# FOX projections of heads 0 to 3 in three panels of 512 features, and the inversions' column steps on GpSimd

## The chip, the core and the metric

The kernel runs on one core of one Trainium2 chip, in one launch. The metric is the device time of that launch in microseconds, as the median of several runs. The engines are TensorE (PE; its weight loads are listed as PEld), VectorE (DVE), ScalarE (ACT), GpSimd (POOL) and SyncE (SP). Each runs its own list of instructions in order and waits on semaphores for the others. DMAs are issued from SP's list (plain loads and stores) and from POOL's (loads that add to what is there).

## What is computed

One decoder block on x of 512 tokens by 1024 features. Two branches run in parallel from u = RMSNorm(x):

```python
proj = rmsnorm(x, g) @ w_in
# A, gated delta rule: 8 heads of 128; q, k, v through a causal conv of 4 and SiLU
#   a_mat = strictly lower part of (beta * k k^T * decay), per chunk
#   sol = triangular_solve(a_mat + eye, [v * beta, k * beta * exp(G)])   # unit lower triangular
#   then a scan over the chunks with state S
# B, forgetting attention (FOX): 8 heads of 128
#   q, k = rmsnorm per head;  p = softmax(q k^T / sqrt(d) + c_t - c_s), causal;  o_b = p v
merged = sigmoid(gate_a) * (y_a @ w_proj_gdn) + sigmoid(gate_b) * (o_b @ w_proj_fox)
h = x + merged @ w_out
out = h + square(relu(rmsnorm(h) @ w_up)) @ w_down
```

All is float32. Each large product is made of three: an operand is split into a high part (`hi`, rounded to the matmul's format) and the rest (`lo`), and hi.hi, lo.hi and hi.lo are added up in PSUM.

## The kernel before

Weights come in units of 128 x 1024 floats (512 KB), in the order of the list `seq`. `load` brings a unit by DMA, `prefetch_split` makes `hi` (ACT, 1.05 us) and `lo` (DVE, 1.22 us) of it, with four buffers for each, and `unit` hands it to the code that multiplies and starts the splits and loads of the next ones.

The stages follow one another: the gates, z and the first delta-rule group (heads 0 to 3, `gdn_group(0)`), the FOX projections of heads 0 to 3 (`fox_pair(0)`, `fox_pair(1)`), the second group (heads 4 to 7), a stream of products that are made by a scheme of seven instead of eight (`stream`, tile `st`, FOX heads 4 to 7 and the gates), the output projections, and the MLP (tile `mlp`), which takes the last 360 us. Small pieces of work run beside them as generators: `head`, `invert`, `scan`, `fox_worker`, `factors_u`. Each `tick()` in the big loops resumes every generator up to its next `yield`. What was written in this order is then put into each engine's list by a scheduler; it may move an instruction to another place in its engine's list, and that list is what the engine runs.

A FOX pair projects q and k of two heads and then v of both, in three panels of 256 features; a panel needs two units. For each block of 128 tokens the weights of TensorE are a block of u (128 x 128) and what streams through is a 256-wide piece of the unit: 24 products a block, 96 a panel, 576 for both pairs (tile `fx`, lines 961, 962, 964). One PSUM bank takes two blocks.

`invert` inverts, for 16 blocks (4 heads x 4 chunks) at once, the unit lower triangular matrices of a group. It starts with the 32 x 32 diagonal blocks: they are transposed on DVE into `E` (line 669), and 31 column steps follow (lines 681, 683): step j multiplies a column of E with a row of X into `tmp` and subtracts that from X, over r x n elements per partition with r = 31 - j and n = j // 2 + 1. Each step needs the one before. Then DVE transposes X back into `Xd` and `XT` (lines 689, 692), and TensorE multiplies the blocks together: `Qp` (line 707), `Tp` and `Tq`, `Q6` and `T6`. The step sizes in `INV_STEP` say how much work of the column steps goes between two ticks. The scan of the group needs the inverse.

POOL has the scalings of FOX q and k (line 889), the power that gives 1/sqrt (346), the masks (878), products for the decays, and the DMA issues of line 219, which add the second and later terms of the stream's and the MLP's weight sums to a buffer already loaded; each of them waits until DVE has made `lo` of what the buffer held.

Of the kernel before, what the change touches and what calls it, by code (L numbers as in the profile page):

```python
# [15 lines left out]
P = 128  # L16
T = 512
# [20 lines left out]
LA_NEW = 7  # L38
LA_RAW = 3
LA_SPLIT = 2  # L40
INV_STEP = (2500, 900)


def hybrid_block(tc, a, out):
# [21 lines left out]
    def nm(s):  # L66
        n_names[0] += 1
        return f"{s}_{n_names[0]}"
# [41 lines left out]
    def cs(c):  # L110
        return slice(c * P, (c + 1) * P)
# [123 lines left out]
    def prefetch_new(n):  # L235

        for m in range(pos[0], min(len(seq), n)):
            if fresh and m not in raws and seq[m][0] in FACTOR and FACTOR[seq[m][0]][1] is None and seq[m][1][0] != "w_st":
                load(m)
            if seq[m] in LONE and m not in begun:  # L240
                begin(m)

    def prefetch_split(n):
        while len(units) < min(len(seq), n):
            raw, cuts = raws[len(units)]
            hi = whl.tile([P, D], F32R, tag="hi", name=nm("hi"))
            if not units:
                h3 = v3(hi[:, 0:512], KT)
                r3 = v3(raw[:, 0:256], KT)
                act.copy(h3[:, :, 0:32], r3)  # L250
                vec.tensor_tensor(h3[:, :, 32:64], r3, h3[:, :, 0:32].bitcast(F32), op=ALU.subtract)
                units.append((hi, None))
                continue
            lo = whl.tile([P, D], F32R, tag="lo", name=nm("lo"))
            for c in cuts:
                act.copy(hi[:, c], raw[:, c])  # L256
                vec.tensor_tensor(lo[:, c], raw[:, c], hi[:, c].bitcast(F32), op=ALU.subtract)  # L257
            units.append((hi, lo))

    def unit(nme):  # L260
        n = pos[0]
        assert seq[n][0] == nme, (seq[n], nme)
        pos[0] += 1
        prefetch_split(n + 1 + LA_SPLIT)
        prefetch_raw(n + 1 + LA_RAW)
        prefetch_new(n + 1 + LA_NEW)
        return units[n]
# [391 lines left out]
    def invert(AT, rest, ahead):  # L659
# [9 lines left out]
        vec.transpose(E_[:, :].rearrange("p (c d i) -> p c d i", c=B, d=2),  # L669
                      dg[:, :].rearrange("p (i c) -> p c i", i=NI).unsqueeze(2).to_broadcast([P, B, 2, NI]))  # L670
        X_ = page(s="X")
        vec.tensor_copy(X_, x_id)
        yield
        E3 = v3(E_[:, :], B)
        X3 = v3(X_[:, :], B)
# [1 line left out]
        for j in range(B - 1):  # L677
            r, n = B - 1 - j, j // 2 + 1
            tmp = smp.tile([P, 144], F32, tag="tmp", name=nm("tmp"), bufs=2)
            t3 = tmp[:, 0:r * n].rearrange("p (a b) -> p a b", a=r)  # L680
            vec.tensor_tensor(t3, E3[:, j + 1:, j:j + 1].to_broadcast([P, r, n]),
                              X3[:, j:j + 1, 0:n].to_broadcast([P, r, n]), op=ALU.mult)
            vec.tensor_tensor(X3[:, j + 1:, 0:n], X3[:, j + 1:, 0:n], t3, op=ALU.subtract)
            w += 2 * (130 + r * n)
            if w > rest:
                w = 0
                yield
# [5 lines left out]
        Xd3 = v3(Xd[:, :], NI)  # L693
        XT3 = v3(XT[:, :], NI)

        X2 = sbp.tile([P, NI, 64], F32, tag="sub", name=nm("X2"))
        pool.memset(X2[0:32, :, 32:64], 0.0)
        act.copy(X2[0:32, :, 0:32], Xd3[0:32, :, :])
# [248 lines left out]
            act.copy(o, po)  # L947
            stores.append(start(store_late(obd[h], o)))

    def fox_pair(hp):  # L950
        vts = ([], [])
        for pn in range(3):
            us = [unit("w_fox"), unit("w_fox")]
            pg2 = [page(s="fqk"), page(s="fqk")]
            for t2 in range(2):
                ps = mmps("fx")
                for tb in (2 * t2, 2 * t2 + 1):
                    o = ps[:, (tb % 2) * 256:(tb % 2 + 1) * 256]
                    for k in range(KT):
                        w = us[k // 4][0][:, (k % 4) * 256:(k % 4 + 1) * 256]  # L960
                        mm(o, uhi[k][:, cs(tb)], w, start=(k == 0), stop=False)  # L961
                        mm(o, ulo[k][:, cs(tb)], w, start=False, stop=False)  # L962
                    for k in range(KT):
                        mm(o, uhi[k][:, cs(tb)], us[k // 4][1][:, (k % 4) * 256:(k % 4 + 1) * 256], start=False,  # L964
                           stop=(k == KT - 1))
                    if tb % 2 == 0:
                        tick()
                if pn < 2:
                    act.copy(pg2[t2], ps)
                else:  # L970
                    for j in range(2):
                        (vec.tensor_copy if j else act.copy)(
                            v3(pg2[j][:, 2 * t2 * P:(2 * t2 + 2) * P], 2), v3(ps[:, :], 2)[:, :, cs(j)])
                tick()
            if pn < 2:
                fq.append((2 * hp + pn, pg2, vts[pn]))
            else:
                for v, x in zip(vts, pg2):
                    v += [x[:, cs(c)] for c in range(NCH)]

    def stream(parts, other):

# [106 lines left out]
    start(decays(0, box, gt))  # L1089
    fws = [start(fox_worker())]  # L1090
    ch0 = gdn_group(0, box)
    fox_pair(0)
    fu = start(factors_u())
    fox_pair(1)
    start(decays(1, box, ch0))
    hold[0] = True
    for h in range(NZ1, H):
# [342 lines left out]
def _layout(inputs):  # L1440
# [18 lines left out]
    o["w_gdn"] = units(qkv)  # L1459
    o["conv"] = c(f["gdn_conv_w"][0].reshape(4, 3, H, P).transpose(3, 2, 1, 0).reshape(P, 24, 4))  # L1460
    fx = w[:, 4112:7184].reshape(D, 3, H, P)
    pan = []
    for hp in range(2):
        for h in (2 * hp, 2 * hp + 1):
            pan.append(np.concatenate([fx[:, 0, h], fx[:, 1, h]], axis=1))
        pan.append(np.concatenate([fx[:, 2, 2 * hp], fx[:, 2, 2 * hp + 1]], axis=1))
    o["w_fox"] = c(np.stack(pan).reshape(6, 2, 4, P, 256).transpose(0, 1, 3, 2, 4).reshape(12, P, D))
    q, k, v = [[fx[:, j, h] for h in range(H)] for j in range(3)]
    st = [np.concatenate(b, axis=1) for b in
          ((v[4], v[5], q[4], k[4]), (q[6], k[6], q[5], k[5]), (q[7], k[7], v[6], v[7]))]  # L1470
# [49 lines left out]
```

## Time and profile before

| what | value |
|---|---|
| median of 3 runs | 983.41 us (983.08 to 984.17) |
| span of the profiled execution, first to last instruction | 980.2 us |
| PE busy | 970.8 us, 99% |
| DVE busy | 710.9 us, 73% |
| ACT busy | 605.0 us, 62% |
| POOL busy | 240.2 us, 25% |
| clock granted to TensorE | full in every slice |
| FOX projections, heads 0 to 3 (`fx`) | from 122.1 to 213.3 us |
| column steps, group 0 and group 1 | 143.5 to 170.4 and 354.4 to 400.1 us, on DVE |

The profile is of one execution; its span ends with the last instruction, and the timed runs are about 3 us longer than it. A row of a group reads: line, engine, operation, output<-inputs with shapes, xcount, then the busy time in us and the mean duration in ns, then the idle time of the engine just before and what ended it. A row of a time line or of the chain reads: start in us, length in us, engine, and what ran. A row of the table by windows reads: window, its length, then busy us and number of instructions of each engine, the clock, the busy share of the DMA engines and GB/s. Matmuls are pipelined, so a recorded duration is longer than the distance from one to the next.

### The profile page before, as it was taken

The numbers are of one execution on the slowest core, as the hardware profiler recorded it, in microseconds if no ns is written. First come the engines' busy times: TensorE is split into PE (matmuls) and PEld (weight loads), VectorE is DVE, ScalarE is ACT, GpSimd is POOL, SyncE is SP. The second block draws the span as 40 slices with busy tenths as digits, with TensorE's granted clock in tenths as the row PEclk, the third lists the DMA queues.
The fourth block names the chain that finished last, engine by engine and source line by source line (L and its number), as shares of the span: only waits on it lengthen the run. The fifth ranks groups of instructions, "written<-read, shape, count | busy, mean of one in ns | idle before, by whom it ended". The sixth has DMA issues, their size and how long they took to land.

```text
span 980.2 us, 17198 instructions
## 1 busy us (share of the span) xinstructions
PE 970.8 (99%) x6545; PEld 874.8 (89%) x6545; DVE 710.9 (73%) x1204; ACT 605.0 (62%) x1050; POOL 240.2 (25%) x236
## 2 busy tenths in 40 slices
PE   8999999999999999999999999999999999999998
PEld 6788899998888999999999888889989989988986
DVE  6877778566577789855656535889896697698596
ACT  7766444766564787867656422678755765666761
POOL 1544120202533513522320005312121121121110
PEclk9999999999999999999999999999999999999999
DMA  7647662475437885757887735688798888889884
GB/s 266 213 135 223 174 158 90 130 239 181 129 116 228 189 166 141 197 129 166 236 201 215 273 103 171 125 181 173 190 188 196 187 173 206 181 175 202 186 166 119
DMA packets 93442, 174.38 MB, mean 178 GB/s; under 512 B 8016, under 2 KB 49200, under 8 KB 93360
## 3 DMA queue, kind: packets, MB, share of 16 engines
q1 hardware_dynamic: 78928, 120.85, 38.8%
q0 software_dynamic: 14432, 52.44, 30.5%
q8 instruction: 51, 0.84, 0.4%
q14 instruction: 31, 0.25, 0.1%
HBM read 152.25 MB, written 21.02 MB: 177 GB/s over the span
## 4 chain that ended last, share of the span: by engine, by line
PE 92%; DVE 4%; DMA 2%; ACT 1%; issue 1%; SPq 0%; DVEq 0%
PE mlp L1171 36%; PE st L1011 12%; PE mm L279 8%; PE mm L276 8%; PE mm L275 8%; PE fx L964 2%; PE fx L961 2%; PE fx L962 2%; PE fo L944 2%; PE sc L919 1%; PE pT L935 1%; DVE lo L257 1%; PE kk L639 1%; PE kq L647 1%; DMA ux<-ud 1%; PE v L797 1%
## 5 line engine op out<-in xcount | busy, mean ns | idle before, releaser
L1402 ACT CAST hi<-draw 128x1024 fp32r<-128x1024 f32 x124 | 130.0, 1050 | 118.4 <-PE mlp L1171 100.4
L1409 DVE TENSOR_TENSOR lo<-draw,hi 128x1024 fp32r<-128x1024 f32 x124 | 151.3, 1222 | 44.8 <-ACT hi L1402 41.6
L256 ACT CAST hi<-raw 128x1024 fp32r<-128x1024 f32 (+1 forms) x62 | 62.9, 1021 | 82.6 <-PE mm L276 59.5
L1171 PE MATMUL mlp<-hi,shi 128*128 128x512 f32 x280 | 109.5, 391 | 0.1
L1171 PE MATMUL mlp<-hi,slo 128*128 128x512 f32 x280 | 109.1, 390 | 0.0
L1171 PE MATMUL mlp<-lo,shi 128*128 128x512 f32 x280 | 109.0, 389 | 0.0
L257 DVE TENSOR_TENSOR lo<-raw,hi 128x1024 fp32r<-128x1024 f32 (+1 forms) x62 | 73.9, 1197 | 29.1 <-ACT hi L256 13.4
L1171 PE MATMUL mlp<-shi,lo 128*128 128x256 f32 x448 | 90.3, 283 | 0.0
L1171 PE MATMUL mlp<-slo,hi 128*128 128x256 f32 x448 | 90.3, 283 | 0.0
L1171 PE MATMUL mlp<-shi,hi 128*128 128x256 f32 x448 | 90.3, 283 | 0.0
L276 PE MATMUL mm<-ulo,hi 128*128 128x512 f32 x216 | 85.0, 394 | 1.2 <-DVE ulo L290 1.2
L275 PE MATMUL mm<-uhi,hi 128*128 128x512 f32 x216 | 85.0, 395 | 0.0
L257 DVE TENSOR_TENSOR lo<-sraw,hi 128x1024 fp32r<-128x1024 f32 x49 | 60.7, 1240 | 20.9 <-ACT hi L256 20.1
L1171 PEld LDWEIGHTS mlp<-shi,hi 128*128 128x128 f32 x448 | 70.6, 192 | 0.9
L1171 PEld LDWEIGHTS mlp<-shi,lo 128*128 128x128 f32 x448 | 69.9, 192 | 0.0
L1171 PEld LDWEIGHTS mlp<-slo,hi 128*128 128x128 f32 x448 | 69.8, 192 | 0.0
L256 ACT CAST hi<-sraw 128x1024 fp32r<-128x1024 f32 x49 | 51.3, 1047 | 26.6 <-PE st L1011 16.2
L1171 PEld LDWEIGHTS mlp<-hi,shi 128*128 128x128 f32 x280 | 52.6, 188 | 11.1 <-issue 0.7
L1171 PEld LDWEIGHTS mlp<-lo,shi 128*128 128x128 f32 x280 | 52.6, 188 | 11.1
L1171 PEld LDWEIGHTS mlp<-hi,slo 128*128 128x128 f32 x280 | 52.6, 188 | 10.3
L219 POOL DMA_DIRECT2D draw<-w_d x30 | 26.3, 876 | 129.9 <-DVE lo L1409 120.8
L219 POOL DMA_DIRECT2D draw<-w_u x32 | 27.7, 866 | 122.6 <-DVE lo L1409 120.0
(336 smaller groups left out, 2466.6 us busy)
## 6 DMA issues: line engine op xcount, KB each, us to landing
draw<-w_u POOLq DMA_DIRECT2D x32, 512.0 KB, 5.7
draw<-w_d POOLq DMA_DIRECT2D x32, 512.0 KB, 6.5
sraw<-w_st POOLq DMA_DIRECT2D x28, 512.0 KB, 5.9
draw<-w_d SPq DMA_DIRECT2D x26, 512.0 KB, 4.4
raw<-w_gdn SPq DMA_DIRECT2D x24, 512.0 KB, 3.8
draw<-w_u SPq DMA_DIRECT2D x24, 512.0 KB, 4.4
sraw<-w_st SPq DMA_DIRECT2D x21, 512.0 KB, 5.5
hd<-hd SPq DMA_DIRECT2D x34, 256.0 KB, 5.4
```

Of the source, the lines that this page charges most:

```text
L219: nc.gpsimd.dma_start(raw, a[w][c, q, s_], accum_op=ALU.add)
L256: act.copy(hi[:, c], raw[:, c])
L257: vec.tensor_tensor(lo[:, c], raw[:, c], hi[:, c].bitcast(F32), op=ALU.subtract)
L275: mm(o, w, rhi(k), start=(k == 0), stop=False)
L276: mm(o, w, rlo(k), start=False, stop=False)
L279: mm(o, lo[:, k * cols:(k + 1) * cols], rhi(k), start=False, stop=(k == KT - 1))
L944: mm(po[:, cs(i)], vt[c], st[i][:, cs(c)], start=(c == 0), stop=(c == i))
L961: mm(o, uhi[k][:, cs(tb)], w, start=(k == 0), stop=False)
L1011: mm(o, u, w, start=first and t == 0 and k == 0 and j == 0 and x is hi, stop=x is lo and k == 3, skip_group_check=True)
L1171: return (lambda *args, **kw: tc.keep_in_program_order(f(*args, **kw))) if self.pinned[0] else f
L1402: pact.copy(hi, raws[m][0])
L1409: pvec.tensor_tensor(lo, raws[m][0], hi[:, :].bitcast(F32), op=ALU.subtract)
```

## The change

The projections of FOX heads 0 to 3 are made in three panels of 512 features: q and k of heads 0 and 1; v of heads 0 to 3; q and k of heads 2 and 3. A panel needs four units, each now two k blocks by 512 features. Two PSUM banks are open at once, one for each of two blocks of 128 tokens; the four units are run through twice, once for each half of the tokens, so all four stay split until the second half has used them. `held` keeps `prefetch_split` from asking for more buffers than are free. A block of tokens takes 24 products of 512 features, a panel 96, all three 288. The bank of a block is copied out by ACT, in two pieces of 256 (q and k) or whole (v). The number of ticks stays 24. `factors_u` now starts after the first of three panels instead of after the first pair.

In `invert` both instructions of every column step go to GpSimd, the first copy of X goes to ACT, there is one more `yield` before `X2`, and the amount of steps between ticks is 1600 for both groups.

```diff
-INV_STEP = (2500, 900)
+INV_STEP = (1600, 1600)
...
+    held = [None]
+
     def prefetch_split(n):
-        while len(units) < min(len(seq), n):
+        while len(units) < min(len(seq), n, len(seq) if held[0] is None else held[0]):
...
         X_ = page(s="X")
-        vec.tensor_copy(X_, x_id)
+        act.copy(X_, x_id)
...
-            vec.tensor_tensor(t3, E3[:, j + 1:, j:j + 1].to_broadcast([P, r, n]),
+            pool.tensor_tensor(t3, E3[:, j + 1:, j:j + 1].to_broadcast([P, r, n]),
                               X3[:, j:j + 1, 0:n].to_broadcast([P, r, n]), op=ALU.mult)
-            vec.tensor_tensor(X3[:, j + 1:, 0:n], X3[:, j + 1:, 0:n], t3, op=ALU.subtract)
+            pool.tensor_tensor(X3[:, j + 1:, 0:n], X3[:, j + 1:, 0:n], t3, op=ALU.subtract)
...
+        yield
         X2 = sbp.tile([P, NI, 64], F32, tag="sub", name=nm("X2"))
...
-    def fox_pair(hp):
...
+    vts = [[] for _ in range(G)]
+
+    def fox_panel(heads):
+
+        n0 = pos[0]
+        held[0] = n0 + 4
+        us = []
+        pgs = {h: [page(s="fqk"), page(s="fqk")] for h in heads}
+        vp = []
+        for half in range(2):
+            ps = {tb: mmps("fx") for tb in (2 * half, 2 * half + 1)}
+            for j in range(4):
+                if not half:
+                    us.append(unit("w_fox"))
+                hi, lo = us[j]
+                for tb, o in ps.items():
+                    for k in (2 * j, 2 * j + 1):
+                        w = hi[:, (k % 2) * T:(k % 2 + 1) * T]
                         mm(o, uhi[k][:, cs(tb)], w, start=(k == 0), stop=False)
                         mm(o, ulo[k][:, cs(tb)], w, start=False, stop=False)
+                for tb, o in ps.items():
+                    for k in (2 * j, 2 * j + 1):
+                        mm(o, uhi[k][:, cs(tb)], lo[:, (k % 2) * T:(k % 2 + 1) * T], start=False, stop=(k == KT - 1))
+                if half:
+                    held[0] = n0 + 5 + j if j < 3 else None
+                    prefetch_split(n0 + 5 + j)
+                    prefetch_raw(n0 + 6 + j)
+                tick()
+            for tb, o in ps.items():
+                if heads:
+                    for i, h in enumerate(heads):
+                        act.copy(pgs[h][half][:, (tb % 2) * 256:(tb % 2 + 1) * 256], o[:, i * 256:(i + 1) * 256])
                 else:
+                    v = page(s="fqk")
+                    act.copy(v, o)
+                    vp.append(v)
+        for h in range(G):
+            vts[h].extend(v[:, cs(h)] for v in vp)
+        for h in heads:
+            fq.append((h, pgs[h], vts[h]))
...
-    fox_pair(0)
+    fox_panel((0, 1))
     fu = start(factors_u())
-    fox_pair(1)
+    fox_panel(())
+    fox_panel((2, 3))
```

The layout of `w_fox` on the host follows the panels. Three places in the engines' lists show what the scheduler makes of it.

On TensorE at the entry to the first group's products Qp, before (`fx` is a bank of the FOX projections, `Xd` the transposed result of the column steps):

```order
L961 MATMUL fx_2168<-hi_1833,uhi_186 128x256
L962 MATMUL fx_2168<-hi_1833,ulo_194 128x256
L964 MATMUL fx_2168<-lo_1828,uhi_179 128x256
L964 MATMUL fx_2168<-lo_1828,uhi_180 128x256
L964 MATMUL fx_2168<-lo_1828,uhi_181 128x256
L707 MATMUL Qp_1875<-Xd_1819,AT_588 32x32
```

and now:

```order
L971 MATMUL fx_1856<-hi_1801,uhi_186 128x512
L972 MATMUL fx_1856<-hi_1801,ulo_194 128x512
L975 MATMUL fx_1856<-lo_1802,uhi_185 128x512
L975 MATMUL fx_1856<-lo_1802,uhi_186 128x512
L710 MATMUL Qp_1808<-Xd_1743,AT_588 32x32
```

Qp stood inside a bank's products and now stands behind a whole bank of them; between the last product kq of the group's heads and the first Qp the list had 283 products of 256 and has 162 of 512. In the second group (`st` are the stream's products) the same stretch had 423 `st` products, 31 `fo`, 32 `pT`, 24 `fqT` and `fkT` and 12 `sc`, and has 290, 26, 25, 8 and 9.

On GpSimd in the second group, before (`sraw` are the adding loads, `conv` a head's q, `fqk` FOX q and k):

```order
L219 DMA sraw_3594<-w_st 128x1024
L652 TENSOR_TENSOR conv_3467<-conv_3467,row_3838 128x512
L219 DMA sraw_4077<-w_st 128x1024
L219 DMA sraw_3594<-w_st 128x1024
L219 DMA sraw_4192<-w_st 128x1024
```

and now, in the same place, with the column steps:

```order
L683 TENSOR_TENSOR tmp_3773<-E_3689,X_3691 128x81
L685 TENSOR_TENSOR X_3691<-X_3691,tmp_3773 128x27x3
L219 DMA sraw_3799<-w_st 128x1024
L683 TENSOR_TENSOR tmp_3838<-E_3689,X_3691 128x78
L685 TENSOR_TENSOR X_3691<-X_3691,tmp_3838 128x26x3
L683 TENSOR_TENSOR tmp_3841<-E_3689,X_3691 128x100
L685 TENSOR_TENSOR X_3691<-X_3691,tmp_3841 128x25x4
L219 DMA sraw_3310<-w_st 128x1024
```

The loads stand between the steps. From the first step to the last the list holds seven of them, two powers, four scalings and one mask in the second group; in the first group one power, two scalings and one mask.

On DVE at the end of the first group's column steps, before:

```order
L681 TENSOR_TENSOR tmp_1790<-E_1537,X_1539 128x16
L683 TENSOR_TENSOR X_1539<-X_1539,tmp_1790 128x16
L689 STREAM_TRANSPOSE Xd_1819<-X_1539 128x32x16
L257 TENSOR_TENSOR lo_2155<-raw_1837,hi_2154 128x1024
L692 STREAM_TRANSPOSE XT_1821<-Xd_1819 128x512
```

and now:

```order
L450 TENSOR_TENSOR ux_1648<-ux_1647,ux_1569 128x256
L450 TENSOR_TENSOR ux_1648<-ux_1647,ux_1571 128x256
L259 TENSOR_TENSOR lo_1700<-raw_1503,hi_1699 128x1024
L259 TENSOR_TENSOR lo_1737<-raw_1601,hi_1736 128x1024
L259 TENSOR_TENSOR lo_1766<-raw_1649,hi_1765 128x1024
L259 TENSOR_TENSOR lo_1802<-raw_1769,hi_1801 128x1024
L691 STREAM_TRANSPOSE Xd_1743<-X_1452 128x32x16
L694 STREAM_TRANSPOSE XT_1745<-Xd_1743 128x512
```

Between E and Xd the list of DVE had four splits of weights `lo` and has eight in the first group; in the second it had fourteen and has eleven.

More of the change, by code (lines that the diff above doesn't have):

```diff
@@ L948, in fox_worker @@
             stores.append(start(store_late(obd[h], o)))
-    def fox_pair(hp):
[L951 to L960, printed above, removed]
+    vts = [[] for _ in range(G)]
@@ L961, in fox_pair @@
                         mm(o, uhi[k][:, cs(tb)], w, start=(k == 0), stop=False)
                         mm(o, ulo[k][:, cs(tb)], w, start=False, stop=False)
[L963 to L969, printed above, removed]
-                else:
-                    for j in range(2):
-                        (vec.tensor_copy if j else act.copy)(
-                            v3(pg2[j][:, 2 * t2 * P:(2 * t2 + 2) * P], 2), v3(ps[:, :], 2)[:, :, cs(j)])
@@ L974, in fox_pair @@
[L974 to L979, printed above, removed]
+                for tb, o in ps.items():
[5 more added lines that the diff above has]
+                    prefetch_raw(n0 + 6 + j)
@@ L1461, in _layout @@
     fx = w[:, 4112:7184].reshape(D, 3, H, P)
[L1462 to L1467, printed above, removed]
+    pan = [np.concatenate([fx[:, j, h] for h in hs for j in js], axis=1)
+           for hs, js in (((0, 1), (0, 1)), (range(4), (2,)), ((2, 3), (0, 1)))]
+    o["w_fox"] = c(np.stack(pan).reshape(3, 4, 2, P, T).transpose(0, 1, 3, 2, 4).reshape(12, P, D))
     q, k, v = [[fx[:, j, h] for h in range(H)] for j in range(3)]
```

## The prediction

> **What bounds the kernel now.** I read the page first, then the waits of TensorE, then the chain that ended last in order of time.
>
> ```profile
> PE 970.8 (99%) x6545; PEld 874.8 (89%) x6545; DVE 710.9 (73%) x1204; ACT 605.0 (62%) x1050; POOL 240.2 (25%) x236
> PE 92%; DVE 4%; DMA 2%; ACT 1%; issue 1%; SPq 0%; DVEq 0%
> PE mm L276 <- DVE ulo L290: 1.2, 2, 0.7
> 144.78 0.96 PE fx L964 x8
> 50.40 1.81 PE mm L279 x8
> 113.39 1.85 PE mm L279 x8
> 324.90 2.87 PE st L1011 x24
> 380.00:390.00 10.00, 10.00 (x81) 9.63 (x80) 9.76 (x28) 6.89 (x15) 1.11 (x2) 1.00 0.54 116
> 390.00:400.00 10.00, 9.83 (x79) 9.15 (x78) 9.76 (x30) 7.65 (x18) 5.64 (x6) 1.00 0.89 187
> 150.00:160.00 10.00, 10.00 (x85) 10.00 (x84) 8.27 (x26) 2.69 (x5) 0.00 (x0) 1.00 0.34 107
> ```
>
> TensorE carries 92% of the chain, and its longest total wait for anyone is 1.2 us. So the time is the sum of TensorE's instructions, and a change helps by shortening that sum or hurts by making TensorE wait. What an instruction costs is its pitch, not its recorded duration: eight 256-wide products take 0.96 us, 0.120 each (24 stream products in 2.87 agree), and eight 512-wide ones 1.81 to 1.85, so 0.226 to 0.231. The last three rows (PE, PEld, DVE, ACT, POOL, clock, DMA) show the one stretch where TensorE is a little thinner, 380 to 400 us, with VectorE at 98%: the second inversion runs there.
>
> **The panels.** Gone are 576 products of 256 features (three groups of 192), come 288 of 512.
>
> ```profile
> L961 PE MATMUL fx<-hi,uhi x192: 278/283/368, 122.4 to 212.1; 128*128 128x256 f32 x192
> L969 ACT COPY fqk<-fx x8: 563/582/590, 128.8 to 205.4; 128x512 f32<-128x512 f32 x8
> L972 ACT COPY fqk<-fx x4: 372/372/375, 155.3 to 215.3; 128x256 f32<-128x256 f32 x4
> L257 DVE TENSOR_TENSOR lo<-raw,hi 128x1024 fp32r<-128x1024 f32 x6 | 7.3, 1217 | 2.3 <-PE fx L964 2.3
> ```
>
> 576 x 0.120 = 69.1 us; 288 x 0.228 = 65.7: a gain of 3.4 (2.6 to 4.0 by the two ends of the pitch). The evictions become sixteen ACT copies of 256 and four of 512, 16 x 0.372 + 4 x 0.582 = 8.3 us where ACT had 8 x 0.582 + 4 x 0.372 = 6.1; ACT is 62% busy and the third bank takes the next token block meanwhile, so I cost this at nothing, and at one copy (0.4) per half panel, 2.4 in all, if that cover is gone. The same twelve units are split, but four stay open per panel, so the next panel's splits fall into its second half, one per twelve products (2.7 us), against 1.22 us of VectorE each: nothing, or 1.2 a panel if VectorE is late.
>
> **The column steps.** Each inversion has 31 steps of two instructions, 62, over 5,712 elements per partition in all (twice the sum of r x n). On VectorE they were:
>
> ```profile
> 141.00:176.00 35.00, 8.61 (x31) 1.00 0.33 95
> 352.00:411.00 59.00, 9.31 (x31) 1.00 0.73 164
> 141.00:176.00 35.00, 7.95 (x31) 1.00 0.33 95
> 352.00:411.00 59.00, 10.83 (x31) 1.00 0.73 164
> 141.07 2.08 DVE L669 STREAM_TRANSPOSE E<-dg 128x1024 f32<-128x1024 f32 x1
> 170.48 1.19 DVE L689 STREAM_TRANSPOSE Xd<-X 128x512 f32<-128x512 f32 x1
> 174.95 1.20 PE L707 MATMUL Qp<-Xd,AT 32*32 32x32 f32 x64
> 351.81 2.11 DVE L669 STREAM_TRANSPOSE E<-dg 128x1024 f32<-128x1024 f32 x1
> 418.64 1.66 PE L707 MATMUL Qp<-Xd,AT 32*32 32x32 f32 x64
> ```
>
> The first two rows are line 681, the next two line 683: 36.7 us leave VectorE. What that gives TensorE is bounded by nothing and by the thin stretch: 81 + 79 instructions in 20 us where 172 would fit, 12 x 0.120 = 1.4 us. I take 1.0.
>
> On GpSimd the price is not in the trace; these are the nearest rows.
>
> ```profile
> 600.67 0.73 POOL L1229 TENSOR_TENSOR m<-gate,gate 128x256 f32<-128x256 f32 x1
> L588 POOL TENSOR_TENSOR eb<-em,row x8: 1272/1292/1533, 77.0 to 295.9; 128x512 f32<-128x512 f32 x8
> L343 POOL TENSOR_SCALAR fqs<-c_fox_q_norm_g 128x1 f32<-128x1 f32 x1 | 0.2, 240 | 12.1 <-DMA c_fox_q_norm_g<-fox_q_norm_g 12.1
> 370.74 1.70 POOL L346 TENSOR_TENSOR fss<-fss,expo 128x8 f32<-128x8 f32 x1 [5.66 <-DVE fsm L931]
> 372.51 1.22 POOL L889 TENSOR_TENSOR fqk<-fqk,fss 128x512 f32<-128x512 f32 x1
> 598.89 1.22 DVE L257 TENSOR_TENSOR lo<-raw,hi 128x1024 fp32r<-128x1024 f32 x1
> 599.06 1.65 POOL L1229 TENSOR_TENSOR m<-gate,gate 128x256 f32<-128x256 f32 x1 [3.10 <-DVE gate L1227]
> 372.55 0.28 DVE L681 TENSOR_TENSOR tmp<-E,X 128x120 f32<-128x120 f32 x1
> 372.86 1.01 DVE L683 TENSOR_TENSOR X<-X,tmp 128x120 f32<-128x120 f32 x1
> ```
>
> A two-input operation takes 0.73 us at 256 elements and 1.29 at 512: 2.2 ns per element and 0.166 fixed. A dependent one follows 0.07 us after its predecessor (372.44 to 372.51). So one inversion costs 62 x 0.236 + 5,712 x 0.0022 = 14.6 + 12.6 = 27.2 us, 0.44 a step. Below, no instruction is cheaper than the 0.240 of the 128x1 operation: 14.9. Above, none costs more than the 256-element one: 62 x 0.73 = 45. I take 27.2, since the steps (16 to 136 elements) lie just under the two rows of their own kind.
>
> The Trainium skill's "GPSIMD Engine Reference" (3.1, elementwise side-by-side cycle accounting) has a two-input operation 1.96 times as long on GpSimd as on VectorE, at 2,048 elements. At 512 elements the trace nearly agrees, 1.29 us in row L588 against 0.69 in this one:
>
> ```profile
> L257 DVE TENSOR_TENSOR lo<-raw,hi 128x512 fp32r<-128x512 f32 x4 | 2.7, 692 | 0.2 <-ACT hi L256 0.2
> ```
>
> By the page's ratio an inversion would take 18.4 x 1.96 = 36 us, an estimate, both chains would be 8.8 us later than in my sum, and the kernel would take 1009 us.
>
> Then the two engines get in each other's way. In the rows above the 256-element operation took 1.65 instead of 0.73 when a VectorE split (two operands in SBUF) had begun 0.17 us earlier, and a 128x120 step on VectorE took 1.01 instead of 0.28 beside a GpSimd operation. So a split costs the GpSimd chain up to 0.92 us, and at least nothing, where GpSimd waits anyway.
>
> **Is it hidden?** Behind the steps stand the transposition Xd (1.19) on VectorE and the products Qp on TensorE, which waits in order; all projections or stream products behind Qp wait with it. GpSimd's own queue adds work between the steps:
>
> ```profile
> L889 POOL TENSOR_TENSOR fqk<-fqk,fss x16: 1032/1057/1346, 142.1 to 442.0; 128x512 f32<-128x512 f32 x16
> L346 POOL TENSOR_TENSOR fss<-fss,expo 128x8 f32<-128x8 f32 x8 | 16.8, 2101 | 57.4 <-DVE fss L885 51.3 <-DVE fsm L931 5.7 <-DVE ssk L620 0.4
> L878 POOL TENSOR_SCALAR_AFFINE_SELECT nd<-row 128x512 f32<-128x512 f32 x8 | 7.7, 958 | 0.0
> L219 POOL DMA_DIRECT2D sraw<-w_st x28 | 24.8, 886 | 94.2 <-DVE lo L257 64.0 <-DVE X L683 12.4 <-DVE fsm L931 9.0
> 135.33 0.89 PE kk L639 x8
> 186.65 1.06 PE sc L919 x2
> ```
>
> First group: before, E ends at 143.2 and Qp starts at 175.0, 31.8 us. Between the last kq product and Qp stood 283 narrow products (34.0 us) and now stand 162 wide ones (36.9), so the room is 34.7. The queue holds one mask (0.96), one power (2.1), two scalings (2.1): 5.2. Eight splits stand on VectorE between E and Xd: 8 x 0.92 = 7.4, taken in full, since GpSimd has no other wait there (the smaller splits and subtractions of the u pages, which now also stand there, I leave out). Sum 27.2 + 5.2 + 7.4 + 1.2 = 41.0: **6.3 us late**.
>
> Second group: 353.9 to 418.6, 64.7 us. The order now has 290 stream products there instead of 423 (16.0 us less), 33 fewer 128-wide records at 0.11 (3.6) and three fewer score products (1.9): room 43.2. The queue holds seven accumulating loads (6.2), two powers (4.2), four scalings (4.2), a mask (1.0): 15.6. Eleven splits, of which I take half of 0.92, since the loads in the queue wait for splits themselves: 5.1. Sum 27.2 + 15.6 + 5.1 + 1.2 = 49.1: **5.9 us late**. The loads come late with the steps; TensorE then waits at a stream unit instead of at Qp, for the same lateness.
>
> **Sum.** -3.4 - 1.0 + 6.3 + 5.9 = +7.8: span 980.2 to 988.0. The median of the runs, 983.4, is 3.2 above the span; I carry that over: **991**. The copy of X to ACT, the extra pause and the step sizes change only the order, which is counted above. A difference under 0.2% (2 us) cannot be told from none.
>
> **Rivals.**
> *The steps are cheap and hidden (faster).* No lateness if an inversion takes at most 34.7 - 13.8 = 20.9 us in the first group and 43.2 - 21.9 = 21.3 in the second, 0.34 us a step. Then 983.4 - 4.4 = 979, or 976 if the thin stretches on either side of the inversion fill too. For it: the 0.240 row, and that the step's broadcast operands may be read faster than the full tiles of the rows. Against it: both two-input rows.
> *No change.* Each microsecond above 21 counts twice; at 23.2 us an inversion (0.375 a step) lateness and gain cancel: 983. A narrow case.
> *GpSimd starves its own loads (much slower).* If an inversion takes 34 us or more and the second group's splits block in full, the sum is (34 + 13.8 - 34.7) + (34 + 27.0 - 43.2) - 4.4 = +26.5: 1010. For it: the load issues wait for VectorE's splits, 64 us in all, and would now stand behind steps that wait too. Against it: in the stage before, those loads land in good time, and POOL is 25% busy.
>
> **How the numbers follow.** Late chains 0.50 (985 to 1001, the price from 24 to 32 us); cheap steps 0.30; no change 0.08; starved loads 0.12. Range 976 to 1007, which leaves out the worst half of the last case and a little of the second; the likeliest case alone gives 985 to 1001. Faster 0.30, same 0.08, slower 0.62.
>
> **What would show it.** Panels: 512-wide products at a pitch of 0.228 and no wait of theirs. Steps: a mean near 0.37 us on GpSimd, the longest near 1.3 where a split runs; the last one about 41 us after E in the first group. Lateness: TensorE's waits headed by Qp for VectorE's Xd, some 6 us twice. I am wrong if a step's mean is under 0.3 us and Qp has no wait, or if the steps are as slow as said and TensorE still does not wait: then the room was larger than the order gives.

## The result and the profile after

| | before | changed |
|---|---|---|
| median of 4 runs | 983.25 us (981.35 to 984.17) | 1020.54 us (1018.66 to 1023.78) |
| ratio | | 1.038, 95% interval 1.036 to 1.040 |
| span of the profiled execution | 980.2 us | 1018.6 us |

The changed kernel is 37 us slower. The prediction, 991 us (976 to 1007), had the direction and a fifth of the size.

From the page of the changed kernel: busy time, the span in 40 slices with the clock in tenths, and the chain that ended last.

```profile
PE 980.4 (96%) x6257; PEld 867.9 (85%) x6257; DVE 681.6 (67%) x1074; ACT 605.9 (59%) x1058; POOL 298.2 (29%) x360
PE   8999998698989999899999999999999999999998
PEclk9999999699989899989999999999999999999999
PE 80%; POOL 6%; DVE 5%; ACT 3%; issue 2%; DMA 2%; SPq 0%; POOLq 0%; DVEq 0%; ACTq 0%
```

TensorE was 92% of the chain and is now 80%. Apart from the first and the last slice, which were thin before too, its thin slices lie between 150 and 440 us, and the slices with a lower clock lie there too. The waits of TensorE and the clock of the whole span:

```profile
PE Qp L710 <- DVE Xd L691: 10.4, 2, 6.9
PE mm L277 <- DVE conv L601: 8.3, 3, 4.2
PE Tp L723 <- ACT Q L713: 5.4, 1, 5.4
PE fo L947 <- ACT pTs L940: 2.8, 1, 2.8
PE mm L277 <- ACT proj L1095: 2.7, 1, 2.7
```

```profile
core 0: 1018.6 us, clock 0.980
```

Before, no line of this list was above 1.2 us and the clock was 1.000. The first line, 10.4 us, is the lateness at Qp that the prediction speaks of. Adding up TensorE's records, its idle time grew from 4.5 to 33.3 us. In the stretches that the clock trace gives as half it was busy for 29.0 us, and half of that, 14.5 us, is an estimate of what the low clock cost (too high where short products are bound by something else). 28.8 + 14.5 is 43.3, and the span grew by 38.4: by this estimate the work itself became some 5 us shorter.

The panels' products, first row and the one twelve products later:

```profile
149.76 0.39 PE L971 MATMUL fx<-hi,uhi 128*128 128x512 f32 x1
...
152.48 0.39 PE L971 MATMUL fx<-hi,uhi 128*128 128x512 f32 x1
```

2.72 us for twelve is 0.227 each, as predicted. The column steps on GpSimd, as groups and in time, with what follows them:

```profile
L683 POOL TENSOR_TENSOR tmp<-E,X 128x126 f32<-128x126 f32 (+22 forms) x62 | 31.2, 504 | 11.3 <-DVE E L671 7.2
L685 POOL TENSOR_TENSOR X<-X,tmp 128x126 f32<-128x126 f32 (+22 forms) x62 | 31.0, 501 | 4.3
```

```profile
141.46 1.08 POOL L683 TENSOR_TENSOR tmp<-E,X 128x31 f32<-128x31 f32 x1 [2.41 <-DVE E L671]
143.83 0.26 POOL L683 TENSOR_TENSOR tmp<-E,X 128x30 f32<-128x30 f32 x1
144.88 1.23 POOL L685 TENSOR_TENSOR X<-X,tmp 128x58 f32<-128x58 f32 x1
180.86 0.22 POOL L685 TENSOR_TENSOR X<-X,tmp 128x16 f32<-128x16 f32 x1
181.11 1.06 DVE L691 STREAM_TRANSPOSE Xd<-X 128x512 f32<-128x512 f32 x1 [7.31 <-POOL X L685]
182.23 1.92 PE L710 MATMUL Qp<-Xd,AT 32*32 32x32 f32 x64 [6.89 <-DVE Xd L691]
190.29 0.26 PE L723 MATMUL Tp<-XT,Q 32*32 32x32 f32 x1 [5.41 <-ACT Q L713]
```

A free step takes 0.2 to 0.5 us, one beside a split 1.1 to 1.5. From the first step to the start of Qp there are 40.8 us, 41.0 were predicted; Qp waits 6.9 us, 6.3 were predicted. But then TensorE has two score products (`sc`) and waits again, 5.4 us, for the copy of Q. ScalarE's list meanwhile:

```profile
184.00 2.50 ACT L715 COPY AT<-XT 32x512 f32<-32x512 f32 x4
186.52 0.62 ACT L288 CAST hi<-ux 128x512 fp32r<-128x512 f32 x1
187.16 1.28 ACT L927 ACT_TABLE_LOAD   x1
...
189.66 0.58 ACT L713 COPY Q<-Qp 32x512 f32<-32x512 f32 x1
```

Before, 28 narrow products lay between Qp and Tp, and Q was copied right behind the AT copies. Here a table load, a softmax and a cast come in between. The table by windows (PE, PEld, DVE, ACT, POOL, clock, DMA, GB/s) shows the second cost of these waits:

```profile
170.00:180.00 10.00, 5.35 (x24) 4.10 (x22) 1.85 (x2) 1.05 (x1) 8.44 (x21) 0.93 0.87 301
180.00:190.00 10.00, 2.64 (x66) 2.28 (x66) 5.18 (x11) 7.64 (x14) 1.30 (x5) 0.50 0.16 60
```

In the clock's own record it falls to one half 3.2 us after the wait at Qp began, and stays there for 17.1 us.

In the second group there are 50.0 us from the first step to the start of Qp (49.1 were predicted), and Qp waits 3.5. Ahead of it, inside that chain, TensorE waits 2.8 us at `fo`, and the cause is a load that GpSimd issues:

```profile
414.67 0.92 POOL L219 DMA_DIRECT2D sraw<-w_st  x1
420.98 1.04 ACT L258 CAST hi<-sraw 128x1024 fp32r<-128x1024 f32 x1 [3.94 <-DMA sraw<-w_st]
422.25 0.49 PE L947 MATMUL fo<-pTs,fqk 128*128 128x128 f32 x2 [2.77 <-ACT pTs L940]
```

The adding load stands in GpSimd's list behind a column step, ScalarE's cast waits 3.9 us for it, and the copy `pTs` that TensorE needs stands behind the cast in ScalarE's list. So some 6.3 us of TensorE's waiting (3.5 and 2.8) belong to the second group's steps, where 5.9 were predicted, and the prediction had said that part of it would move to a load. The wait at `fo` of 2.4 us or more, behind such a cast (3.2 to 4.6 us), is there in every kernel below that has the second group's steps on GpSimd together with the small edits, and in neither kernel that has the changed kernel's other edits and these steps on VectorE.

### The profile page after: what moved, and what is told of

Its sections match the earlier page's. It is cut to its first block, busy times and chain, and to the rows that moved or that the text cites. A ratio compares the mean times of both kernels' runs of the same rounds, so it can differ in the third digit from the quotient of the medians.

```text
span 1018.6 us, 16633 instructions
## 1 busy us (share of the span) xinstructions
PE 980.4 (96%) x6257; PEld 867.9 (85%) x6257; DVE 681.6 (67%) x1074; ACT 605.9 (59%) x1058; POOL 298.2 (29%) x360
## 4 chain that ended last, share of the span: by engine, by line
PE 80%; POOL 6%; DVE 5%; ACT 3%; issue 2%; DMA 2%; SPq 0%; POOLq 0%; DVEq 0%; ACTq 0%
PE mlp L1185 34%; PE st L1024 9%; PE mm L277 8%; PE mm L278 7%; PE mm L281 7%; POOL X L685 3%; POOL tmp L683 3%; PE fo L947 1%; PE sc L922 1%; PE fx L971 1%; PE fx L975 1%; PE fx L972 1%; DVE conv L601 1%; DMA row<-obd 1%; ACT hi L258 1%
## 5 line engine op out<-in xcount | busy, mean ns | idle before, releaser
L277 PE MATMUL mm<-uhi,hi 128*128 128x512 f32 x216 | 89.3, 415 | 11.0 <-DVE conv L601 8.3
L278 PE MATMUL mm<-ulo,hi 128*128 128x512 f32 x216 | 89.1, 413 | 1.1 <-DVE ulo L292 1.1
```

Of the source, the lines that this page charges most:

```text
L277: mm(o, w, rhi(k), start=(k == 0), stop=False)
L278: mm(o, w, rlo(k), start=False, stop=False)
```

## The experiments

Ratios are to runs of the kernel before on the same chip. "Half clock" is the estimate above, "idle" TensorE's idle time in the records (before: 4.5). These two columns are of the one profiled execution, which took 1011.6 us for panels + small edits and 995.5 us for small edits alone, 5 to 6 us over their medians; there they are high.

| kernel | median us | ratio (95%) | more than before | idle | half clock |
|---|---|---|---|---|---|
| panels alone | 995.74 | 1.013 (1.012 to 1.015) | 12.9 | 16.2 | 3.6 |
| steps on GpSimd alone | 992.14 | 1.009 (1.008 to 1.011) | 9.3 | 9.9 | 4.7 |
| small edits alone | 989.51 | 1.007 (1.004 to 1.010) | 6.7 | 12.7 | 6.8 |
| panels + GpSimd | 1008.92 | 1.027 (1.025 to 1.028) | 26.1 | 28.5 | 7.2 |
| panels + small edits | 1006.21 | 1.024 (1.020 to 1.028) | 22.7 | 22.5 | 16.1 |
| GpSimd + small edits | 1007.17 | 1.024 (1.021 to 1.026) | 23.7 | 21.1 | 5.7 |
| all (the change) | 1020.54 | 1.038 (1.036 to 1.040) | 37.3 | 33.3 | 14.5 |

The small edits are the step sizes 1600 and 1600, the pause ahead of `X2`, and the first copy of X on ScalarE. Theory A is that the late column steps make the loss, B that the panels carry part of it, D that the small edits do.

**Panels and small edits, steps on VectorE.**

```diff
-            pool.tensor_tensor(t3, E3[:, j + 1:, j:j + 1]...
+            vec.tensor_tensor(t3, E3[:, j + 1:, j:j + 1]...
-            pool.tensor_tensor(X3[:, j + 1:, 0:n], ...
+            vec.tensor_tensor(X3[:, j + 1:, 0:n], ...
```

> The changed kernel with both instructions of every column step back on VectorE; the panels, the held buffers, the copy of X on ACT, the extra pause and the step sizes stay. Theory A (the late column steps alone make the loss, and what follows them): 980 us (976 to 985), TensorE at full clock throughout, no wait at Qp over 1 us. Theory B (the panels, with four units held split, push splits and late work aside and so carry part of the loss): over 990, with waits between 280 and 340 us still there.

1006.2 us: theory A falls. Without a single step on GpSimd the kernel loses 22.7 of the 37.3 us. Waits of TensorE in this kernel:

```profile
PE mm L277 <- DVE conv L601: 7.8, 3, 4.3
PE Tp L723 <- ACT Q L713: 6.3, 1, 6.3
PE Qp L710 <- DVE Xd L691: 2.8, 2, 1.9
```

The waits at Tp and at the second group's projections are those of the changed kernel; the wait at Qp is smaller, and the one at `fo` is gone.

**Steps on GpSimd and small edits, panels of 256.** The kernel before, and of the change only:

```diff
-INV_STEP = (2500, 900)
+INV_STEP = (1600, 1600)
...
-        vec.tensor_copy(X_, x_id)
+        act.copy(X_, x_id)
...
-            vec.tensor_tensor(t3, ...
+            pool.tensor_tensor(t3, ...
-            vec.tensor_tensor(X3[:, j + 1:, 0:n], ...
+            pool.tensor_tensor(X3[:, j + 1:, 0:n], ...
...
+        yield
         X2 = sbp.tile(...
```

> The kernel before with the column steps on GpSimd, the copy of X on ACT, the extra pause and the step sizes 1600; the projections stay in panels of 256. Theory A: as late as in the changed kernel, 1015 to 1027 us, since only 3.4 us of panels are missing. Theory B: under 1005, since what the panels push aside stays where it was.

1007.2 us, between the two: the panels are not the only other cause either, since the waits of the convolutions (8.6 us in all) are here without them.

**Only one group's steps on GpSimd.**

```diff
-    def invert(AT, rest, ahead):
+    def invert(AT, rest, ahead, eng):
...
-            pool.tensor_tensor(t3, ...
+            eng.tensor_tensor(t3, ...
-            pool.tensor_tensor(X3[:, j + 1:, 0:n], ...
+            eng.tensor_tensor(X3[:, j + 1:, 0:n], ...
```

`eng` is GpSimd for one group and VectorE for the other.

> The changed kernel with only the first group's column steps on GpSimd. TensorE loses some 21 us more than before up to 240 us, and 13 between 280 and 340, both ahead of the second inversion; if all of it comes from the first group's lateness (theory A), 1010 us (1004 to 1016) and the waits of line 277 for line 601 stay. By my prediction's sum (6.3 late, nothing behind it) it would be 986.

> The changed kernel with only the second group's column steps on GpSimd. Theory A: the losses at 400 to 440 us remain, some 10 us, so 990 us (985 to 995), and nothing is lost before 380 us. By my prediction's sum (5.9 late): 985. If the losses at 280 to 340 us come from the panels or the second group itself, over 998.

1012.3 and 1012.2 us. Above the 1006.2 with neither, the first group costs 6.1 us and the second 6.0; my sum had 6.3 and 5.9. The runs with neither lie between 1002.7 and 1011.6 us, so that each of the two costs is uncertain by several us and the closeness is partly luck. The waits agree better than that: with the first group's steps on GpSimd TensorE waits 9.0 us at Qp instead of 2.8, with the second group's 4.7, and 2.7 more at `fo` and 1.4 at `fqT`. Both groups together cost 14.3. So the price of the steps was sized well, given the order, and the larger loss, which the prediction lacks, is in the 22.7 us of the other parts.

**The three parts alone.** Four more kernels complete the eight combinations. Their edits to the kernel before: the panels (`fox_panel` and `held`, as in the change); the two lines of the steps; the other three pieces of the last diff; and the panels with the two lines.

> The kernel before with only the panels of 512; the inversion as before. Theory B: over 1000, with the waits at 280 to 340 us. Theory D: those waits are gone. In TensorE's list the first group's room is 28.0 us of products where it was 35.7, so Qp may be some 7 us late, which with the lower clock behind an idle stretch makes 990 (985 to 997). By my prediction's terms for the panels alone: 980.

> The kernel before with only the column steps on GpSimd; step sizes, pause and copy as before. Room in TensorE's list 38.5 us in the first group and 57.3 in the second, against some 40 and 49 us of steps as measured in the changed kernel. Theory D: the first group some 3 us late, the second not at all: 988 us (983 to 994). Theory A: 1005 or more, since the steps are as slow as in the changed kernel.

> The kernel before with only the three small edits to the inversion: step sizes 1600 and 1600, the extra pause, the first copy of X on ScalarE; steps on VectorE, panels of 256. Theory D (these edits, which my prediction counted only through the room, move the products that cover the inversions: the second group's room from the last kq product to Qp falls from 59.0 to 41.9 us of products in TensorE's list): 1000 to 1007 us, with the waits of the convolutions between 280 and 340 us. Theories A and B: 981 to 985.

> The changed kernel without the three small edits: panels of 512 and column steps on GpSimd, step sizes 2500 and 900. Room 28.0 us in the first group, so Qp is some 11 us late there, and 57.3 in the second, where nothing waits. Theory D: 995 to 1003 with full clock after 250 us and no waits of the convolutions. Theory A: 1015 or more.

Each part loses by itself; alone they add up to 28.9, together they take 37.3. No theory had all four. The panels alone (995.7) and the steps alone (992.1) lie in theory D's ranges, high in both; the small edits alone (989.5) lie between D and the other two; panels + GpSimd (1008.9) lie above D and below A. And the second group waited for GpSimd where room was enough. Waits of TensorE, the panels alone:

```profile
PE Qp L709 <- DVE Xd L691: 4.9, 1, 4.9
PE fx L970 <- ACT fqk L986: 3.0, 1, 3.0
```

With step size 2500 the scheduler leaves 114 panel products between the last kq product and Qp, 26.0 us at 0.228, where before there were 283 of 256 features, 34.0 us at 0.120: even VectorE's steps come late. And TensorE waits for a bank of the panel to be copied out. The steps alone:

```profile
PE fqT L898 <- POOL fqk L889: 4.2, 1, 4.2
PE Tp L720 <- ACT Q L710: 2.0, 1, 2.0
```

Qp waits 0.5 us here. What is late is GpSimd's other work, the scaling of FOX q and k, behind the steps. The small edits alone:

```profile
PE mm L275 <- DVE conv L599: 5.4, 2, 3.2
PE mm L275 <- ACT gate L992: 2.0, 1, 2.0
```

They touch only the inversion, yet they make TensorE wait at the projections of the second group, at 291 and 309 us (the wait for `gate` lies at 537 us). The reason can be followed in the line of the decays' exponentials (minimum, median and maximum duration, first and last start), before and with the small edits:

```profile
L578 ACT ACTIVATE em<-D x8: 592/598/601, 63.4 to 272.8; 128x512 f32<-128x512 f32 x8
```

```profile
L578 ACT ACTIVATE em<-D x8: 592/598/600, 63.7 to 287.3; 128x512 f32<-128x512 f32 x8
```

`decays(1, box, ch0)` starts when the first group's scan has ended. Smaller steps and one more pause take more ticks (which of the three edits does it was not tried apart), the scan ends later, and the exponentials, with two loads of ScalarE's table (1.28 us each), move from behind 12, 12, 15 and 15 convolution evictions to behind 14, 14, 16 and 16.

**Decays that don't wait for the scan** (the changed kernel otherwise).

```diff
-    start(decays(1, box, ch0))
+    start(decays(1, box))
```

> The changed kernel with one line different: the decays of the second group no longer wait for the first group's scan to end (in ScalarE's list their four exponentials then stand behind 12, 12, 13 and 13 convolution evictions; in the changed kernel 14, 14, 16, 16, before 12, 12, 15, 15). If the decays, pushed into the second group's projections, make the waits at 280 to 340 us, the 13.2 us lost there go: 1007 us (1003 to 1011). If the late scan's own copies on ScalarE make them, they stay: 1015 or more.

1015.6 us: 4.9 us came back. By its number this is the second expectation (1015 or more), but two of the three waits are gone:

```profile
PE mm L277 <- DVE conv L601: 3.6, 1, 3.6
```

```profile
283.61 0.58 ACT L823 COPY om<-o 128x512 f32<-128x512 f32 x1 [3.30 <-PE o L821]
284.09 0.69 ACT L598 ACTIVATE conv<-mm,c_conv 128x512 f32<-128x512 f32 x1
```

In ScalarE's list the eviction of line 598 stands behind the copy of the scan's last output, which waits 3.3 us for TensorE. So the decays made two of the waits, and the late scan itself the third (read from these rows, not tried). Between 280 and 340 us TensorE's loss (distance to the next product beyond the median of its kind, added up) fell from 15.4 to 7.3 us; part of the gain was lost again in the second group.

**The second group's step size at 900.**

```diff
-INV_STEP = (1600, 1600)
+INV_STEP = (1600, 900)
```

> The changed kernel with the second group's step size back at 900 (1600, 900): in TensorE's list 56.8 us of products instead of 41.9 stand ahead of Qp there, against 48.8 us of steps on GpSimd. If the step size, and not GpSimd's speed, makes the second group late, the 10 us lost at 400 to 440 us go: 1010 us (1006 to 1013). If GpSimd's accumulating loads are what is late, they stay: 1016 or more.

1016.9 us: the second expectation. Waits of TensorE:

```profile
PE Qp L710 <- DVE Xd L691: 6.9, 1, 6.9
PE fqT L901 <- POOL fqk L892: 3.7, 4, 1.7
PE fo L947 <- ACT pTs L940: 2.4, 1, 2.4
```

The second group's wait at Qp is gone (one of two is left), and waits for the scalings on GpSimd have come instead: the steps' room was not all that GpSimd lacked. The expectation named the loads. That is half of it: the wait at `fo` stands again behind a cast that waits 3.2 us for such a load, and the 3.7 us at `fqT` are the scalings.

**Filling the wait.** In the kernel with panels and steps on GpSimd, TensorE waits 13.0 us at Qp. Here 52 products, which nobody needs, stand ahead of it.

```diff
+NFILL = 52
...
+        if not inverted[0]:
+            for _ in range(NFILL):
+                mm(pqs[0], uhi[0][:, 0:P], uhi[0][:, 0:T], start=True, stop=True)
```

> The kernel with panels of 512 and steps on GpSimd but without the small edits (1008.9 us), where TensorE waits 13.0 us at the first group's Qp and then runs 10.7 us more at half clock. Ahead of Qp stand 52 additional products of 512 into Qp's own bank, whose result is overwritten: 11.9 us at full clock. If the low clock is a consequence of the idle stretch, it goes, and the kernel is faster with more work: 1003.5 us (1001 to 1006). If it has another cause, or costs nothing: 1009 or more.

1008.5 us against 1008.9: 11.9 us of useless products cost nothing, and gain nothing to speak of. The windows without and with them:

```profile
170.00:180.00 10.00, 0.50 (x18) 0.50 (x20) 1.58 (x2) 0.52 (x1) 7.24 (x22) 0.50 0.00 0
180.00:190.00 10.00, 7.00 (x67) 5.72 (x63) 6.15 (x12) 8.44 (x14) 0.00 (x0) 0.50 0.01 2
```

```profile
170.00:180.00 10.00, 7.97 (x94) 6.35 (x93) 2.41 (x4) 1.86 (x4) 6.07 (x19) 1.00 0.01 2
180.00:190.00 10.00, 6.96 (x21) 5.58 (x22) 5.18 (x8) 7.52 (x11) 0.00 (x0) 0.66 0.14 43
```

The clock stays full until 180 us: the low clock does follow from idleness. Of the expected 5 us some 3 came, by the estimate of half clock (7.2 us without, 4.0 with): the next wait, 3.7 us for a bank, then brings the clock down on its own. What came was mostly lost again in longer waits, 6.2 us instead of 4.6 for GpSimd's scalings at `fqT` and 3.7 instead of 3.0 for the bank.

**Panels, with room.** Two tries at an order in which the panels wait for nothing, both with the steps on VectorE. The first is the panels alone with another step size and free decays:

```diff
-INV_STEP = (2500, 900)
+INV_STEP = (1300, 900)
...
-    start(decays(1, box, ch0))
+    start(decays(1, box))
```

> Panels of 512 with the column steps on VectorE, step sizes 1300 and 900, no extra pause, and the second group's decays not waiting for the scan. In TensorE's list 39.0 us of products stand ahead of the first Qp (28.0 in the panels alone), 8.8 between Qp and Tp, 59.0 in the second group. If the panels lose only by the order that they bring, all waits go and their 3.4 us remain: 980 us (978 to 984). If holding four units split or the evictions cost by themselves: 987 or more.

1004.4 us, a miss, by one wait more than by anything else:

```profile
PE mm L277 <- DVE conv L601: 10.3, 2, 9.1
```

The first inversion got its room, by more ticks, and the scan came later still (its last output at 273.9 us, in the panels alone at 261.7). In the trace VectorE's convolutions stand behind the norm and the scalings of the next head, from 293.3 to 299.4 us; that head's transposes on TensorE come right behind the one of the scan's last output. The second kernel has one more tick per unit, so that the inversion can have many small pieces and still end early (the steps then on GpSimd too, for comparison):

```diff
-INV_STEP = (2500, 900)
+INV_STEP = (400, 900)
...
+                tick()
                 for tb, o in ps.items():
                     for k in (2 * j, 2 * j + 1):
                         mm(o, uhi[k][:, cs(tb)], lo[...
```

> The panels alone (995.7 us) with one more tick for every unit, after its products with the high part, and the first group's step size at 400. In TensorE's list 46.9 us of products then stand ahead of the first Qp, 3.8 between Qp and Tp and 59.0 in the second group, and the second group's decays behind 12, 12, 13 and 13 convolution evictions, so that both the first inversion and the scan's end have room. If the panels lose only by the order that they bring, every wait over 1 us goes and 3.4 us of shorter products remain: 980 us (977 to 983). If they have a price of their own (evictions, held splits): 986 or more.

> The same with the column steps on GpSimd: 46.9 us of products stand ahead of the first Qp for some 41 us of steps, 57.3 in the second group for 49. If lateness at Qp is all that GpSimd costs, it equals the one with the steps on VectorE, 980 us (977 to 984). If GpSimd's other work (scalings of FOX q and k, powers) comes late behind the steps, as in the steps on GpSimd alone (wait of 4.2 us at the transposes fqT): 987 to 995.

998.7 and 1002.6 us. Qp, Tp and the convolutions no longer wait in either, so the order did what was asked; the panels still lose 15.9 us, and GpSimd 3.9 more, at fqT (4.7 us) as expected of its own price. In the profiled execution of the first, 11.2 us of this are idle time and 5.1 half clock, and TensorE's work is 1.0 us longer than before instead of 3.4 shorter; why is not shown. What the panels wait for (waits of TensorE, then ScalarE's list, steps on VectorE):

```profile
PE fx L970 <- ACT fqk L987: 6.0, 2, 3.2
```

```profile
164.25 1.28 ACT L926 ACT_TABLE_LOAD   x1
...
168.79 0.62 ACT L288 CAST hi<-ux 128x512 fp32r<-128x512 f32 x1
169.32 1.07 ACT L987 COPY fqk<-fx 128x512 f32<-128x512 f32 x2
```

The half panel ended at 164.3 us, and its two banks are copied out at 169.3, behind a softmax, casts of u and a table load. Three runs asked why.

```diff
-                        act.copy(pgs[h][half]...
+                        vec.tensor_copy(pgs[h][half]...
-                    act.copy(v, o)
+                    vec.tensor_copy(v, o)
```

> The panels with a tick more per unit and step size 400 (998.7 us), with the copies of the panels' banks on VectorE instead of ScalarE. TensorE waits there twice 3 us at line 970 for a copy that stands in ScalarE's list behind the softmax of a FOX head and the casts of the u pages. If it is that place in ScalarE's list, the two waits and the half clock behind them go: 990 us (986 to 993). If VectorE's list, which carries the column steps there, is as late, nothing changes: 997 or more.

```diff
-NMM = 3
+NMM = 4
```

> The same (998.7 us) with four banks instead of three for the large products, and four instead of five for the small ones. Two banks open at once then leave two free ones for the next half panel, and no product needs a copy that has just been asked for. If the panels' own price is that two of three banks end together, the waits at line 970 go: 990 us (986 to 993). If small products wait for the bank that they lose: 997 or more.

```diff
                 for tb, o in ps.items():
                     for k in (2 * j, 2 * j + 1):
                         w = hi[...]
...
-                for tb, o in ps.items():
                     for k in (2 * j, 2 * j + 1):
                         mm(o, uhi[k][:, cs(tb)], lo[...
+                    if tb % 2 == 0:
+                        tick()
```

The additional tick then stands behind the first bank's six products.

> The panels with a tick more per unit and step size 400 (998.7 us), and of each unit first all six products of the one bank and then all six of the other, where now the four high products of both come first. The first bank then ends six products ahead of the second instead of two, and the second bank of the next half is asked for six products after the first instead of four: 1.4 us more for the copy that TensorE waits 3 us for. If the panels' own price is that wait for a bank: each wait some 1.4 us shorter, and with less half clock 993 us (990 to 996). If the copy is late for what stands ahead of it in ScalarE's list, however early the bank ends: 997 or more.

997.9, 1016.9 and 998.7 us. On VectorE the copies wait as long (7.0 us in two), behind steps and softmax there. With a fourth bank no product of the panels waits over 0.5 us for a bank any more, and the five waits of the convolutions (10.2 us) and four of the softmax transposes (7.1) that come instead cost more. Bank by bank, nothing changed, and the row says why:

```profile
169.22 1.06 ACT L987 COPY fqk<-fx 128x512 f32<-128x512 f32 x2
```

The first bank was done earlier and was copied out when ScalarE's list got there, at 169.2. So the rows point to the place of the copies in the list. Moving them to the front of ScalarE's list was not tried, and the 6.0 us of these two waits, with the half clock behind them, are only part of the 15.9. No kernel here beats the one before.

## Why the prediction was wrong, step by step

*The panels (-3.4).* The products' size was right: 0.227 us. The step that failed stands behind it: the evictions, which the sum takes "at nothing", and at worst "at one copy (0.4) per half panel", 2.4 us in all. For a single late eviction TensorE waited 2.8 to 3.2 us, since it is not the copy's length that counts but what stands ahead of it on ScalarE. That the panels also leave fewer products ahead of Qp I had counted only as room for GpSimd's steps; alone, at step size 2500, VectorE's steps are late in it too. Panels alone: +12.9 instead of -3.4.

*"The copy of X to ACT, the extra pause and the step sizes change only the order, which is counted above."* This sentence failed most. The order was counted at two places, Qp in each group. The same edits move the end of the scan, the decays and the copies of Q: +6.7 us alone, and with the panels +22.7, at places that the prediction never looked at (Tp 6.3, the convolutions 7.8 us).

*VectorE's relief (-1.0).* The some 5 us by which the work got shorter leave room for it, but no run measured it apart; the same estimate gives 2.0 us for the panels alone.

*The price of the steps (+6.3, +5.9).* Right in the mechanism, and in size for the order that was counted: 6.9 us of waiting at Qp in the first group, and in the second 3.5 at Qp and 2.8 behind a late load. The straight line through 256 and 512 elements held for the small steps too: it gives 0.20 us at 16 elements and 0.465 at 136, and the fastest ones took 0.215 and 0.448. Splits block a step up to 1.5 us, as said. The mean of 0.50 us is above the 0.37 that I gave, because I left the blocked steps out of the mean. The ratio of 1.96 from the Trainium skill's "GPSIMD Engine Reference" (3.1) was too dear: by it the first chain would have taken 50 us, and it took 40.8. Missed was that the steps delay the scalings that stand behind them on GpSimd: 1.4 to 6.2 us at fqT in the runs that have this wait, even where Qp hardly waits (0.5 us at Qp and 4.2 at fqT in the steps alone). One reading was loose, though nothing in the sum rests on it: the 128x120 step of 0.28 us also ran while GpSimd's scaling, recorded from 372.51 us, was under way.

*A wait costs its length.* No step says so, and all count so; in the changed kernel the half clock behind 28.6 us of waits over 1 us cost up to 14.5 more.

*The rivals.* "Cheap steps" and "no change" are out by the step's price. "GpSimd starves its own loads" (1010) came nearest in time and is mostly wrong in its cause: a late load stands behind the 2.8 us at `fo` and behind none of the other waits over 2 us. The range ended where its worst half began; a case with several waits at once had no place in it.

In numbers: my 988.0 of span had 12.2 us of late steps, and 13.2 came (10.4 at Qp, 2.8 at `fo`), 1.0 more. With 16.4 us of other waits (8.3 for convolutions, 5.4 at Tp, 2.7 for an eviction of line 1095) and 14.5 of half clock this makes 1019.9; the span is 1018.6.

## What to carry to other kernels

Where one engine is 99% busy because a scheduler has fitted everything else around it, an edit's price is not its instructions but the waits that it opens: look up, in the new lists, what stands ahead of every copy that frees a PSUM bank and of every producer of the next product, also two stages on, where a chained task (here decays behind a scan) ends later. Count a product's wait from the list of the engine that feeds it, and add the clock that a stretch of a few idle microseconds takes away. Undo an edit's small companions one by one: here three lines about pauses and step sizes lost 6.7 us alone, and 10 to 14 on top of either large part.

## What the runs showed of the hardware

TensorE's clock halves behind a wait. In all profiles here, no idle stretch under 1.3 us (from 20 us on) was by itself followed by a lower clock, every one over 3.5 us was, or lay in one, and between them most; the shortest that was, with no second wait soon behind it, had 1.71 us, while one of 3.24 us was not. The clock fell 2 to 5 us after the stretch began (sooner where another lay ahead), to 0.50, and stayed there for 3.4, 6.8, 10.2, 13.7, 17.1 or 20.5 us, multiples of 3.4, so that by the estimate of half the busy time 2 us of waiting could cost 3.7 or more. The Trainium skill's "TensorE: Matmul & The Clock Gate" (Part 1, the HAM clock gate) tells of a free-running window of about 3.4 us by which the clock is set to half or full; the lengths agree with it, and so does that the same wait halves the clock in one kernel and not in another (3.17 us of waiting near 330 us did in the changed kernel, and did not with the second group's step size at 900). It gives at least one idle window as the condition, and the stretches of 1.7 to 3.3 us here are shorter than that.

GpSimd and VectorE block each other in both directions. In the changed kernel the two 128x31 steps at the start of the chain took 1.08 and 1.13 us while VectorE made two splits (141.25 to 143.63 us), and the 128x30 one behind them 0.26; and in the small edits alone VectorE's 128x4 products took up to 1.25 us beside GpSimd's 128x512 products of the decays, 0.15 without.
